# A list schedule with other durations and other ranks, in a two-layer trunk on one core

## Chip, core and metric

The kernel runs on one core of one Trainium2 chip. A core has five engines that each work through a queue of their own in program order: TensorE (PE; its weight loads are listed apart as PEld), VectorE (DVE), ScalarE (ACT), GpSimd (POOL) and SyncE (SP), which here issues nearly all DMAs. Engines wait for one another by semaphores. The metric is the device time of one execution in microseconds; lower is better.

## What is computed

Two layers over 1024 tokens of width 1024, each with three branches that share one input product, and then an output product and a gated addition:

```python
for i in range(2):
    z = rms_norm(x, norm_g[i]) @ w_in[i]
    z_a, z_b, z_c = split_cols(z, (1664, 936, 1536))
    y_a = rwkv7_branch(z_a, ...)      # a recurrence over tokens, 6 heads of 64
    y_b = dsa_branch(z_b, ...)        # the 256 best keys of each query, then attention over them, 4 heads
    y_c = dilated_branch(z_c, ...)    # banded attention at three rates, 2 heads each, joined by their lse
    x = x + concatenate([y_a, y_b, y_c]) @ w_out[i]
    gate = sigmoid(rms_norm(x, ple_norm_g[i]) @ ple_w_gate[i])
    x = x + gate * (p[i] @ ple_w_proj[i])
return rms_norm(x, final_norm_g)
```

The recurrence, per token and head, is `state = state * w + sa (kk * a) + v k`, with `sa = state @ -kk`. In `dsa_branch` the selection is a `top_k` of index scores `sum_h relu(iq_h . ik) * iw_h`.

## The kernel before

Each layer has a head (norm, transposes, the first columns of the input product), a middle that holds the three branches, and a tail (the output product and the gate). Head and tail are written out in order. The middle is not: it is some 120 Python generators ("streams"), each of which yields pieces of work, and `Flow.run` decides at build time in which order their instructions are put into the engines' queues. What it emits is fixed; nothing is rescheduled on the chip.

A stream yields `piece(engine, us)` ahead of the instructions that this piece issues, `get`/`put` for buffers (slots) that limit how far streams may run ahead, and `after`/`done` for events. `Flow.run` keeps a clock per engine. It takes the piece that can start earliest by that clock, and among pieces that can start at the same time the one of the lowest rank:

```python
self.streams.sort(key=lambda st: st["rank"])
...
start = lambda st: max(st["ready"], self.free.get(st["want"][1], 0.0))
st = min(ready, key=start)
_, engine, us, aside = st["want"]
end = self.free[engine] = start(st) + us
st["end"] = end + self.gap(st, engine)
```

`gap` is what a handover is taken to cost: one number between two pieces of a stream on one engine, and `LATENCY[engine]` from one engine to another. So the durations in the `piece` calls, the gaps and the ranks set the order, and only the order.

The streams that the change and the prediction speak of, by the lines of the profile:

- **z products** (`z_streams`, L728 to L730): the rest of the input product, 720 groups of three matmuls per layer, two PSUM banks. A bank is emptied by ACT and DVE (L748, L750, L753 for the RWKV columns, L762, L768 to L771 for the others) and then stored. Products have rank 50, the evictions 1.5. Their weights are split in two halves by ACT (L682) and POOL (L694).
- **Search** (`dsa_select`): 34 rounds of a bit-wise search for the 256th best key. A round counts keys under a threshold, for four query blocks on DVE (L572) and two on ACT (L555), and then updates the threshold on DVE (L577 to L579). Ranks 7 and, for ACT's counts, 6.
- **Mask** (`dsa_mask`, L623 to L636): six blocks of DVE work that turn the result into an additive mask, stored to DRAM. Rank 7. Its end closes the memory pools of the search; the dilated attention opens in their place.
- **RWKV**: the tokens in eight chunks (hf 0 to 7) of 128. A chunk has a preparation (`rwkv_prep`, rank 4: L1239 to L1326), products between its tokens (`rwkv_cross`, L1372 and L1376), an inverse (`rwkv_inverse`, rank 2) whose core is 31 columns of two dependent DVE operations each (L1451, L1454) that end in a transpose XT (L1462), a merge on PE (L1487, L1499), two chain steps through the state (`rwkv_chain`, rank 0: L1532 to L1559), and an output (`rwkv_out`, L1618 to L1648). Buffers hold two chunks' inverses at a time.
- **Dilated attention** (`dil_att`, from L1040 on, 24 units) with its join (`dil_join`, L1148 to L1183), and **attention over the selected keys** (`dsa_attend`, L905 to L985, ranks 29 to 34), which begins when the mask and all z products are done.
- **embedded** (rank 60, L327 to L329 into `a`): products for the tail's gate, which fill PE.

The tail (`tail`, L327 to L329 into `z`) follows the last row of the middle in each queue.

Of the kernel before, what the change touches and what calls it, by code (L numbers as in the profile page):

```python
# [34 lines left out]
RW, DS, DL = 0, 1664, 2600  # L35

# [85 lines left out]
class Flow:  # L122
# [3 lines left out]
    LATENCY = dict(PE=0.25, ACT=0.2, DVE=0.22, POOL=0.2, SP=2.4)  # L126
# [70 lines left out]
def tile_kernel(ctx, tc, x, p, norm_g, w_in, tshift_mu, rwkv_w0, rwkv_w_up, rwkv_a0, rwkv_a_up, rwkv_k_k,  # L197
# [149 lines left out]
    def dsa_index(flow, ix, zk, zp, sp_, ZT, d):  # L347
# [17 lines left out]
        def kv():  # L365
            for tp in range(0, NT, 2):
# [3 lines left out]
                for (_, zz), nm, half in zip(parts, "ri", (8, 4)):  # L370
                    yield piece("POOL", 1.0)
# [3 lines left out]
                yield piece("DVE", 0.1, True)  # L375
                DVE.tensor_scalar(iw[:, tp:tp + 2], z[:, :, 160:168], 1 / 16.0, None, OP.mult)
                yield piece("ACT", t_act(256) + t_act(128))
# [5 lines left out]
                yield piece("POOL", t_pool(128) + t_pool(64))  # L383
# [8 lines left out]
                yield piece("ACT", t_act(256))  # L392
# [19 lines left out]
        def iq():  # L412
            for tp in range(2, NT, 2):
                z = ZT["iq", tp].rearrange("p t (h e) -> p t h e", e=32)
                yield piece("POOL", 1.6)
# [7 lines left out]
                for e in range(2):  # L423
                    yield get("iqS")
                    iqS = IQ[tp + e] = ix.tile([96, 8, 128], F32R, name="iqS", bufs=2)
                    for j in range(2):
# [5 lines left out]
                        yield piece("ACT", t_act(512))  # L432
# [4 lines left out]
        def products(u):  # L437
# [6 lines left out]
            yield piece("PE", 0.02 + (c.stop - c0) / 2400)  # L444
# [5 lines left out]
        def relus(u):  # L450
            yield get("rl")
            n = B[u].shape[1]
            yield piece("ACT", 0.05 + n / 1200)
# [4 lines left out]
        def sums(u):  # L458
# [4 lines left out]
            yield piece("DVE", 0.12 + (c.stop - c0) / 960)  # L463
# [16 lines left out]
        def keys():  # L480
            for qb in range(2, NT):
# [3 lines left out]
                yield piece("ACT", 2 * t_act(n))  # L485
# [3 lines left out]
                yield piece("DVE", t_dve(n) + 0.3)  # L489
# [5 lines left out]
        def q():  # L495
            yield after("rwkv")
            ka = d["ka"]
            for tp in range(0, NT, 2):
# [5 lines left out]
                yield piece("ACT", t_act(512))  # L504
# [5 lines left out]
                for j in range(2):  # L510
# [7 lines left out]
                    yield piece("ACT", t_act(512))  # L518
# [8 lines left out]
        for g in (kv(), iq()):  # L527
            flow.add(1.7, g)
        flow.line("index", units, (2.0, products), (1.9, relus), (1.8, sums))
        flow.add(1.8, keys())  # L530
        flow.add(2.1, q())


    def dsa_select(add, mk, d):
# [13 lines left out]
        def act_counts():  # L548
            for i in range(counts):
                lower = i // (counts // 2)  # L550
                yield after("t", i)
                for qb in on_act:
                    n = (qb + 1) * 128
                    yield piece("ACT", 0.19 + n / 1080)
# [4 lines left out]
        def search():  # L559
# [7 lines left out]
            for i in range(counts):  # L567
                lower, bit = i // (counts // 2), 15 - i % (counts // 2)
                for qb in range(2, NT - COUNT_ACT):
                    n = (qb + 1) * 128  # L570
                    yield piece("DVE", 0.08 + n / 1750)
# [3 lines left out]
                yield piece("DVE", 0.35)  # L575
# [8 lines left out]
                else:  # L584
# [8 lines left out]
                    for qb in range(2, NT):  # L593
                        hi, lo = hl[qb]
                        yield piece("DVE", t_dve(200 * (qb + 1)))
# [6 lines left out]
        add(7, search())  # L602
        add(6, act_counts())

    def dsa_mask(mk, d):
# [11 lines left out]
        for qb in range(2, NT):  # L617
            n, j = (qb + 1) * 128, slice(qb - 2, qb - 1)
            hi, lo = d["hl"][qb]
            yield piece("DVE", t_dve(n))  # L620
# [4 lines left out]
            yield piece("DVE", t_dve(1.5 * n))  # L625
            DVE.tensor_tensor(bias, bias, tmp, OP.mult)
            DVE.tensor_tensor_scan(tmp, zero.to_broadcast([128, n]), bias, need[:, j], OP.add, OP.subtract)
            yield piece("DVE", t_dve(n))
            DVE.tensor_scalar(tmp, tmp, 0.0, None, OP.is_ge)
            DVE.tensor_tensor(bias, bias, tmp, OP.mult)  # L630
            for src, lim in ((hi, T), (lo, t)):
                yield piece("DVE", t_dve(n))
                DVE.tensor_scalar(tmp, src, lim[:, j], None, OP.is_gt)
                DVE.tensor_tensor(bias, bias, tmp, OP.add)
            yield piece("DVE", t_dve(n / 2))
# [1231 lines left out]
```

## Time and profile before

| | |
|---|---|
| median of three runs | 1970.13 us (1969.46 to 1970.62) |
| the profiled execution, its own time | 1973.16 us |
| its span, first to last instruction | 1971.4 us |
| PE, DVE, ACT, POOL busy, share of the span | 92%, 70%, 53%, 30% |
| middle of layer 0 | search 170 to 390, mask 395 to 483, last z product 636, first matmul of the tail 793.9 |
| middle of layer 1 | search from 1146, mask to 1456, last z product 1604, first matmul of the tail 1766 |

The spans of busy time are of one execution. Matmuls are pipelined and their ends are modelled, so a PE that reads as busy may still have room; the time from the start of one matmul to that of the next in a full stretch tells what one costs. The two layers run the same program and look alike in the trace.

### The profile page before, as it was taken

What the parts mean: (1) busy time and instruction counts of PE and PEld (TensorE: products, weight loads), DVE (VectorE), ACT (ScalarE), POOL (GpSimd) and SP (SyncE); (2) the same over time, 40 slices, a digit from 0 to 9 for tenths busy, and PEclk for the clock granted to TensorE, in tenths of its full rate; (3) what the DMA queues carried; (4) which work ended last, traced back from release to release, by engine and by line L of the source; (5) the groups of instructions that cost most, each with busy time, mean ns of one, the idle gap of its engine ahead of it and who ended that gap; (6) DMA issues with size and microseconds to landing.
All of it is one profiled execution on the core that took longest, in us unless ns stands there. A gap on an engine that the chain in (4) does not pass through costs nothing. (4 is left out here: it accounts for less than half of the span.)

```text
span 1971.4 us, 38650 instructions
## 1 busy us (share of the span) xinstructions
PE 1823.1 (92%) x14062; PEld 1666.9 (85%) x14062; DVE 1382.3 (70%) x3676; ACT 1054.1 (53%) x2393; POOL 593.8 (30%) x810
## 2 busy tenths in 40 slices
PE   7999888899999999899999988888889999999998
PEld 6887677888898888799998876787889988889998
DVE  4479999999788774215345899999996878732344
ACT  4576666543566676214246766665336667652323
POOL 5422144253222222223225212433442222212322
PEclk9999998999999999899999999989989989999999
DMA  5212232223233455612322223222242344464123
GB/s 188 70 58 82 72 96 81 64 74 111 75 99 99 146 146 160 203 44 65 108 93 69 70 73 88 79 76 67 83 118 62 106 120 135 130 197 136 47 81 114
DMA packets 232407, 196.23 MB, mean 100 GB/s; under 512 B 19284, under 2 KB 204056, under 8 KB 232216
## 3 DMA queue, kind: packets, MB, share of 16 engines
q1 hardware_dynamic: 232216, 193.75, 32.6%
q8 instruction: 111, 1.82, 0.4%
q14 instruction: 80, 0.66, 0.1%
HBM read 128.32 MB, written 65.37 MB: 98 GB/s over the span
## 5 line engine op out<-in xcount | busy, mean ns | idle before, releaser
L728 PE MATMUL z<-wH,HT 128*128 128x256 f32 x1024 | 318.8, 311 | 5.8 <-DVE zt L750 3.7
L729 PE MATMUL z<-wL,HT 128*128 128x256 f32 x1024 | 300.6, 294 | 1.3 <-POOL wL L694 1.3
L730 PE MATMUL z<-wH,LT 128*128 128x256 f32 x1024 | 299.7, 293 | 0.0
L329 PE MATMUL z<-wH,LT 128*128 128x256 f32 x1024 | 293.4, 288 | 4.1 <-DVE LT L238 4.1
L327 PE MATMUL z<-wH,HT 128*128 128x256 f32 x1024 | 290.9, 286 | 5.4 <-ACT HT L237 5.4
L328 PE MATMUL z<-wL,HT 128*128 128x256 f32 x1024 | 292.5, 287 | 0.0
L694 POOL TENSOR_TENSOR wL<-wraw,wH 128x512 fp32r<-128x512 f32 (+1 forms) x128 | 169.9, 1332 | 364.9 <-ACT wH L682 311.0
L728 PEld LDWEIGHTS z<-wH,HT 128*128 128x128 f32 x1024 | 207.2, 202 | 12.9 <-DVE zt L750 4.1
L729 PEld LDWEIGHTS z<-wL,HT 128*128 128x128 f32 x1024 | 207.5, 203 | 1.8 <-POOL wL L694 1.7
L730 PEld LDWEIGHTS z<-wH,LT 128*128 128x128 f32 x1024 | 206.6, 202 | 0.0
L329 PEld LDWEIGHTS z<-wH,LT 128*128 128x128 f32 x1024 | 198.3, 194 | 6.3 <-DVE LT L238 6.3
L327 PEld LDWEIGHTS z<-wH,HT 128*128 128x128 f32 x1024 | 198.1, 194 | 6.3 <-ACT HT L237 6.3
L328 PEld LDWEIGHTS z<-wL,HT 128*128 128x128 f32 x1024 | 198.7, 194 | 0.2
L319 POOL TENSOR_TENSOR wL<-wraw,wH 128x512 fp32r<-128x512 f32 (+1 forms) x72 | 100.3, 1413 | 295.7 <-ACT wH L318 292.5
L728 PE MATMUL z<-HT,wH 128*128 128x512 f32 x416 | 169.0, 406 | 18.0 <-DVE zt L750 9.5
L729 PE MATMUL z<-LT,wH 128*128 128x512 f32 x416 | 165.0, 397 | 0.0
L730 PE MATMUL z<-HT,wL 128*128 128x512 f32 x416 | 164.6, 396 | 0.0
L1451 DVE TENSOR_TENSOR xt<-AT,X 128x48 f32<-128x48 f32 (+20 forms) x496 | 135.7, 277 | 8.1
L1454 DVE TENSOR_TENSOR X<-X,xt 128x48 f32<-128x48 f32 (+20 forms) x496 | 124.4, 255 | 7.4
L318 ACT CAST wH<-wraw 128x512 fp32r<-128x512 f32 (+1 forms) x72 | 46.7, 652 | 133.5 <-PE z L329 92.0
L572 DVE TENSOR_SCALAR_CACHE_REDUCE junk<-hi,t 128x384 bf16<-128x384 uint16 (+3 forms) x136 | 110.4, 812 | 4.3
L728 PEld LDWEIGHTS z<-HT,wH 128*128 128x128 f32 x416 | 79.7, 192 | 38.2 <-DVE zt L750 12.0
(287 smaller groups left out, 4548.5 us busy)
## 6 DMA issues: line engine op xcount, KB each, us to landing
wraw<-in_w_in_dram SPq DMA_DIRECT2D x208, 128.0 KB
zr<-zt SPq DMA_DIRECT2D x52, 256.0 KB
zd<-zt SPq DMA_DIRECT2D x48, 256.0 KB
z<-zd SPq DMA_DIRECT2D x48, 256.0 KB
pd<-pe SPq DMA_DIRECT2D x32, 256.0 KB
wraw<-in_w_out_dram SPq DMA_DIRECT2D x32, 256.0 KB
hn<-yT SPq DMA_DIRECT2D x16, 512.0 KB
wraw<-in_ple_w_gate_dram SPq DMA_DIRECT2D x32, 256.0 KB
```

The costliest lines, as they stand in the source:

```text
L318: ACT.copy(H[:, :, :n], raw)
L319: POOL.tensor_tensor(L[:, :, :n], raw, H[:, :, :n].bitcast(F32), OP.subtract)
L327: PE.matmul(o, aH, bH, start=j == 0, stop=False)
L328: PE.matmul(o, aH, bL, start=False, stop=False)
L329: PE.matmul(o, aL, bH, start=False, stop=j == n - 1)
L572: DVE.tensor_scalar(junk[0][:, :n], hl[qb][lower], col(t, qb), None, OP.is_lt, OP.add, accum_out=col(cnt, qb))
L694: POOL.tensor_tensor(L, RAW.pop(it), H.bitcast(F32), OP.subtract)
L728: PE.matmul(o, aH, bH, start=k == 0, stop=False)
L729: PE.matmul(o, aH, bL, start=False, stop=False)
L730: PE.matmul(o, aL, bH, start=False, stop=k == 7)
L1451: DVE.tensor_tensor(tmp, AT[:, j + 1:, j:j + 1].rearrange("p t o -> p o t").to_broadcast([128, m, n]), X[:, :m, j:j + 1].to_broadcast([128 ...
L1454: DVE.tensor_tensor(X[:, :m, j + 1:], X[:, :m, j + 1:], tmp, OP.add)
```

## The change

A table of ranks, `RANK`, is set at the head of the file, and the streams take their rank from it. With it `search`, `counts` (ACT's part of the search) and `mask` get rank -1, ahead of all others, where they had 7, 6 and 7; the other ranks keep their values. The durations in some ninety `piece` calls and the gaps get other numbers. No instruction is added or removed, on any engine. Line numbers of the changed kernel are four to five higher.

```diff
+RANK = dict(chain=0, merge=1, inverse=2, cross=3, tokens=3, ahead=3, prep=4, y=5, out=6, counts=-1, search=-1, mask=-1,
+            products=50, evict=1.5, weights=1.6, embed=60, kept=35, columns=1.7, index=2.0, q=2.1, load=10, dil=20,
+            join=19, dsa=30)
...
-    LATENCY = dict(PE=0.25, ACT=0.2, DVE=0.22, POOL=0.2, SP=2.4)
+    LATENCY = dict(PE=0.2, ACT=0.14, DVE=0.12, POOL=0.13, SP=2.4)
...
-        return 0.13 if st["want"] and st["want"][0] == "piece" and st["want"][1] == engine else self.LATENCY[engine]
+        return 0.11 if st["want"] and st["want"][0] == "piece" and st["want"][1] == engine else self.LATENCY[engine]
...
-                    yield piece("DVE", 0.08 + n / 1750)
+                    yield piece("DVE", 0.17 + n / 960)
...
-                yield piece("DVE", 0.35)
+                yield piece("DVE", 0.9)
...
-        add(7, search())
-        add(6, act_counts())
+        add(RANK["search"], search())
+        add(RANK["counts"], act_counts())
...
-                        yield piece("PE", 0.645, True)
+                        yield piece("PE", 0.7, True)
...
-                yield piece("DVE", t_dve(m * n))
+                yield piece("DVE", 0.13 + m * n / 500)
...
-                yield piece("DVE", t_dve(m * n))
+                yield piece("DVE", 0.13 + m * n / 800)
...
-            flow.add(7, dsa_mask(mk, d))
+            flow.add(RANK["mask"], dsa_mask(mk, d))
```

What this does to the queues is shown at three places of layer 0's middle.

DVE's queue about the last z eviction of the RWKV columns (L750), on which the RWKV preparation waits, before. `hi_613` to `hi_619` are the keys of four query blocks, `cnt` the counts, `t` the threshold; the rows from L585 on begin the second half of the search:

```order
L572 TENSOR_SCALAR junk_634,cnt<-hi_613,t 128x384
L572 TENSOR_SCALAR junk_634,cnt<-hi_615,t 128x512
L572 TENSOR_SCALAR junk_634,cnt<-hi_617,t 128x640
L572 TENSOR_SCALAR junk_634,cnt<-hi_619,t 128x768
L750 SCALAR_TENSOR_TENSOR zt<-z,prm,zt 128x511
L585 TENSOR_TENSOR lim<-lim,cnt 128x6
L587 TENSOR_SCALAR lim<-lim 128x1 x6
L588 TENSOR_SCALAR T<-t 128x6
```

The same eviction in the changed kernel, where it is L754, the counts are L576 and the updates L581 to L583:

```order
L581 TENSOR_TENSOR step<-cnt,lim 128x6
L582 TENSOR_SCALAR step<-step 128x6
L583 TENSOR_TENSOR t<-t,step 128x6
L754 SCALAR_TENSOR_TENSOR zt<-z,prm,zt 128x511
L576 TENSOR_SCALAR junk_634,cnt<-hi_613,t 128x384
L576 TENSOR_SCALAR junk_634,cnt<-hi_615,t 128x512
L576 TENSOR_SCALAR junk_634,cnt<-hi_617,t 128x640
L576 TENSOR_SCALAR junk_634,cnt<-hi_619,t 128x768
```

The eviction moved ahead by four rounds of the search: before it stood behind the counts of all 17 rounds of the first half, now it stands behind those of 13.

DVE's queue where the columns of RWKV chunk 1 end (XT, L1462) and the mask's first block (L623 to L627) begins, before:

```order
L1451 TENSOR_TENSOR xt<-AT_1924,X 128x16
L1454 TENSOR_TENSOR X<-X,xt 128x8x2
L1618 TENSOR_REDUCE ost<-Yt 128x6
L1619 SCALAR_TENSOR_TENSOR Yt<-ost,Yt 128x384
L1451 TENSOR_TENSOR xt<-AT_1924,X 128x8
L623 TENSOR_SCALAR junk_634<-hi_613,T 128x384
L624 TENSOR_SCALAR junk_635<-lo_614,t 128x384
L1454 TENSOR_TENSOR X<-X,xt 128x8
L626 TENSOR_TENSOR junk_634<-junk_634,junk_635 128x384
L627 SCALAR_TENSOR_TENSOR junk_635<-zero,lim,junk_634 128x384
L1462 STREAM_TRANSPOSE XT<-X 128x256
```

The end of the mask's last block (`hi_623`, L640) in the changed kernel, where the same columns (now L1456 and L1459, on `AT_1898`) are at the tenth of 31, and an eviction of a late z product (L775, before L771) stands close by:

```order
L634 TENSOR_TENSOR junk_634<-junk_634,junk_635 128x1024
L1456 TENSOR_TENSOR xt<-AT_1898,X 128x69
L637 TENSOR_SCALAR junk_635<-hi_623,T 128x1024
L638 TENSOR_TENSOR junk_634<-junk_634,junk_635 128x1024
L1459 TENSOR_TENSOR X<-X,xt 128x3x23
L637 TENSOR_SCALAR junk_635<-lo_624,t 128x1024
L638 TENSOR_TENSOR junk_634<-junk_634,junk_635 128x1024
L1456 TENSOR_TENSOR xt<-AT_1898,X 128x66
L640 TENSOR_SCALAR hi_623<-junk_634 128x1024
L1459 TENSOR_TENSOR X<-X,xt 128x3x22
L1291 SCALAR_TENSOR_TENSOR kh<-zk,prm,t 128x128 x3
L775 SCALAR_TENSOR_TENSOR zt<-zt,z 128x2x128
```

The whole mask moved from behind chunk 1's columns to ahead of them, and 15 of the 16 evictions of L771 stand ahead of chunk 1's XT, where 4 stood before.

PE's queue at the end of the middle, before: the last transposes and values of the attention (L940, L963), its output (L982), and then the tail:

```order
L940 MATMUL a<-cst,pr 128x128 x4
L963 MATMUL a<-v,pT 128x64 x16
L982 MATMUL a<-cst,y 128x128 x2
L327 MATMUL z<-wH,HT 128x256
L328 MATMUL z<-wL,HT 128x256
```

And in the changed kernel, where the 24 transposes of the join stand just ahead of these rows: the merge of the last RWKV chunk (L1492, L1504), its two chain steps (L1537 to L1582), its output (L1643), and then the tail (L331):

```order
L1492 MATMUL t<-XN,G 32x32 x12
L1504 MATMUL t<-TT,rs 32x32 x12
L1537 MATMUL a<-S_1900,AR 128x128 x3
L1550 MATMUL a<-rs,TT 64x64 x6
L1560 MATMUL a<-SV,BKt 128x128 x3
L1582 MATMUL a<-SV,G 64x64 x6
L1537 MATMUL a<-S_1901,AR 128x128 x3
L1550 MATMUL a<-rs,TT 64x64 x6
L1560 MATMUL a<-SV,BKt 128x128 x3
L1582 MATMUL a<-SV,G 64x64 x6
L1643 MATMUL t<-cst,o_9179 128x128 x3
L331 MATMUL z<-wH,HT 128x256
```

The last chunk of the recurrence now ends the middle with nothing between its steps; before, attention rows stood between and behind them.

## Rows read from the trace of the kernel before

**Rows 1.** The page: busy time of each engine, and DVE's and PE's busy tenths in 40 slices of 49.3 us.

```profile
PE 1823.1 (92%) x14062; PEld 1666.9 (85%) x14062; DVE 1382.3 (70%) x3676; ACT 1054.1 (53%) x2393; POOL 593.8 (30%) x810
PE   7999888899999999899999988888889999999998
DVE  4479999999788774215345899999996878732344
```

**Rows 2.** Busy time by stretch, layer 0: the first half of the search, the second half and the mask, from there to the XT of RWKV chunk 7, from there to the tail's first matmul; and sums of these.

```profile
core 0: us, PE busy (x) PEld busy (x) DVE busy (x) ACT busy (x) POOL busy (x), PEclk, DMA share, GB/s
170.00:254.00 84.00, 72.09 (x324) 57.99 (x322) 77.58 (x203) 53.88 (x97) 18.93 (x24) 0.98 0.27 79
254.00:491.00 237.00, 206.13 (x1713) 195.94 (x1714) 224.71 (x649) 119.11 (x260) 91.79 (x130) 0.91 0.28 81
491.00:726.60 235.60, 223.69 (x2121) 204.21 (x2119) 186.75 (x656) 152.18 (x449) 56.00 (x72) 0.96 0.36 108
726.60:793.90 67.30, 64.89 (x521) 53.78 (x520) 30.63 (x86) 42.55 (x90) 16.22 (x18) 0.99 0.53 161
170.00:793.90 623.90, 566.80 (x4675) 511.92 (x4673) 519.66 (x1591) 367.72 (x895) 182.93 (x244) 0.95 0.34 100
```

**Rows 3.** The same for the answering stretches of layer 1.

```profile
1229.00:1464.00 235.00, 202.36 (x1714) 192.39 (x1715) 225.45 (x653) 119.52 (x261) 93.50 (x130) 0.93 0.29 83
1464.00:1699.00 235.00, 222.93 (x2116) 203.75 (x2115) 185.89 (x653) 152.22 (x449) 55.72 (x72) 0.96 0.36 107
```

**Rows 4.** What PE waited for between 170 and 254 us: us in total, times, longest.

```profile
PE z L728 <- DVE last L753: 5.3, 4, 2.5
PE z L728 <- DVE zt L750: 4.8, 3, 1.7
```

**Rows 5.** DVE's groups between 170 and 390 us (busy us, mean ns | idle before), those of the search and of RWKV's columns.

```profile
L572 DVE TENSOR_SCALAR_CACHE_REDUCE junk<-hi,t 128x384 bf16<-128x384 uint16 (+1 forms) x68 | 55.2, 812 | 2.1
L1451 DVE TENSOR_TENSOR xt<-AT,X 128x60 f32<-128x60 f32 (+24 forms) x55 | 15.7, 287 | 0.3
L1454 DVE TENSOR_TENSOR X<-X,xt 128x60 f32<-128x60 f32 (+24 forms) x54 | 14.3, 267 | 0.3
```

**Rows 6.** PE in two stretches of 25 us that it filled, with z products 512 wide and with products 256 wide: the count of matmuls stands behind its busy time.

```profile
150.00:175.00 25.00, 25.00 (x111) 20.47 (x110) 22.07 (x33) 17.00 (x29) 7.01 (x13) 1.00 0.28 83
850.00:875.00 25.00, 25.00 (x211) 25.00 (x210) 2.95 (x5) 3.99 (x7) 6.70 (x6) 1.00 0.13 43
```

**Rows 7.** The z products of L728 alone (one of the three matmuls of a group) from 170 us on: PE and PEld busy with them, and counts.

```profile
170.00:254.00 84.00, 41.54 (x108) 20.50 (x107) 0.98 0.27 79
254.00:491.00 237.00, 114.91 (x370) 76.16 (x370) 0.91 0.28 81
491.00:640.00 149.00, 40.26 (x127) 24.74 (x126) 0.95 0.31 92
```

**Rows 8.** The XT of RWKV chunks 1 and 4: start, duration, engine, line.

```profile
397.38 0.42 DVE L1462 STREAM_TRANSPOSE XT<-X 128x256 f32<-128x256 f32 x1
580.88 0.45 DVE L1462 STREAM_TRANSPOSE XT<-X 128x256 f32<-128x256 f32 x1
```

**Rows 9.** RWKV chunk 7 from its XT to its last row, in order of time: start, duration, engine, line (other rows between them left out).

```profile
726.12 0.45 DVE L1462 STREAM_TRANSPOSE XT<-X 128x256 f32<-128x256 f32 x1
...
732.00 0.63 ACT L1503 COPY TT<-t 32x192 f32<-32x192 f32 x2
...
737.27 0.89 PE L1532 MATMUL a<-S,AR 128*128 128x128 f32 x6
...
743.32 0.74 DVE L1559 TENSOR_TENSOR S<-a,sp 64x192 f32<-64x192 f32 x2 [0.34 <-PE a L1555]
...
746.40 0.94 PE L1532 MATMUL a<-S,AR 128*128 128x128 f32 x6
...
752.38 0.74 DVE L1559 TENSOR_TENSOR S<-a,sp 64x192 f32<-64x192 f32 x2 [0.24 <-PE a L1555]
753.15 0.56 DVE L1579 TENSOR_TENSOR Yt<-a,rs 64x384 f32<-64x384 f32 x1
...
758.48 0.56 DVE L1632 TENSOR_TENSOR o<-Yt,ost 128x384 f32<-128x384 f32 x1
...
761.13 0.50 PE L1638 MATMUL t<-cst,o 128*128 128x128 f32 x3
...
764.19 0.55 DVE L1648 SCALAR_TENSOR_TENSOR o<-o,zg 128x384 f32<-128x384 f32 x1
```

**Rows 10.** The end of the middle and the tail's first matmuls, in order of time.

```profile
792.46 0.37 ACT L985 COPY yt<-a 128x256 f32<-128x256 f32 x1 [4.30 <-PE a L982]
793.85 0.58 PE L327 MATMUL z<-wH,HT 128*128 128x256 f32 x1 [1.43 <-ACT HT L237]
797.20 0.41 PE L329 MATMUL z<-wH,LT 128*128 128x256 f32 x1
797.41 0.41 PE L327 MATMUL z<-wH,HT 128*128 128x256 f32 x1
...
800.55 0.28 PE L328 MATMUL z<-wL,HT 128*128 128x256 f32 x1
800.67 0.28 PE L329 MATMUL z<-wH,LT 128*128 128x256 f32 x1
```

**Rows 11.** DVE's columns of one chunk, and POOL, about 552 us; and POOL's splits of z weights (L694) between 491 and 640 us: busy time and count.

```profile
551.61 0.21 DVE L1451 TENSOR_TENSOR xt<-AT,X 128x30 f32<-128x30 f32 x1
551.85 0.19 DVE L1454 TENSOR_TENSOR X<-X,xt 128x30 f32<-128x30 f32 x1
552.08 0.97 DVE L1451 TENSOR_TENSOR xt<-AT,X 128x29 f32<-128x29 f32 x1
553.08 0.19 DVE L1454 TENSOR_TENSOR X<-X,xt 128x29 f32<-128x29 f32 x1
552.00 1.00 POOL L1645 TENSOR_TENSOR o<-o,t 128x384 f32<-128x384 f32 x1 [3.39 <-ACT o L1641]
491.00:640.00 149.00, 8.30 (x6) 0.95 0.31 92
```

More of the change, by code (lines that the diff above doesn't have):

```diff
@@ L527, in dsa_index @@
         for g in (kv(), iq()):
[L528 to L531, printed above, removed]
+            flow.add(RANK["columns"], g)
+        flow.line("index", units, *((RANK["index"] - 0.1 * k, f) for k, f in enumerate((products, relus, sums))))
+        flow.add(RANK["index"] - 0.2, keys())
+        flow.add(RANK["q"], q())
     def dsa_select(add, mk, d):
@@ L993, in dsa_attend @@
         units = [(qb, h, c0) for qb in range(NT) for h in range(4) for c0 in range(0, (qb + 1) * 128, 512)]
-        flow.line("qload", range(NT), (10, load))
-        flow.line("dsa", units, (32, scores), (33, biased), (30, softmax))
-        flow.line("dsb", units, (31, transposes), (31, turned), (34, values))
-        flow.line("dso", range(NT), (29, output))
+        flow.line("qload", range(NT), (RANK["load"], load))
+        flow.line("dsa", units, *((RANK["dsa"] + k, f) for k, f in ((2, scores), (3, biased), (0, softmax))))
+        flow.line("dsb", units, *((RANK["dsa"] + k, f) for k, f in ((1, transposes), (1, turned), (4, values))))
+        flow.line("dso", range(NT), (RANK["dsa"] - 1, output))
     hrow = lambda h: slice(h % 2 * 64, h % 2 * 64 + 64)
@@ L1128, in output @@
                 yield done("dil")
-        flow.line("dil", units, (10, load), (24, turn), (24, turned), (23, scores), (23, biased), (22, softmax),
-                  (21, transposes), (21, weights), (20, values), (20, output))
+        flow.line("dil", units, (RANK["load"], load), *((RANK["dil"] + k, f) for k, f in (
+            (4, turn), (4, turned), (3, scores), (3, biased), (2, softmax), (1, transposes), (1, weights), (0, values),
+            (0, output))))
     def dil_join(opened):
@@ L1268, in icl @@
             lora, wa, ta, ke = R["lora"], T["wa"], tile_("ta"), tile_("ke")
-            yield from product(lambda pr: lora[64:, fc(pr)], lambda pr: wa[64:], "ACT", 3 * t_act(128), tanh(ta, "a0"))
-            yield piece("DVE", 3 * t_dve(128) + t_dve(384))
+            yield from product(lambda pr: lora[64:, fc(pr)], lambda pr: wa[64:], "ACT", 0.8, tanh(ta, "a0"))
+            yield piece("DVE", 1.6)
             for pr in range(3):
@@ L1643, in rwkv_out @@
         yield put("t")
-        yield piece("POOL", t_pool(384))
+        yield piece("POOL", 1.07)
         POOL.tensor_tensor(dv, dv, R["t2"], OP.add)
         yield put("t2")
-        yield piece("DVE", t_dve(384))
+        yield piece("DVE", 0.52)
         DVE.scalar_tensor_tensor(dv, dv, 0.5, g, OP.mult, OP.mult)
```

194 lines of the change are left out of this document (97 added, 97 removed).

## The prediction

> **What bounds the kernel now.** I read the page first. PE is busy for 92% of the span, but DVE's tenths show where the kernel changes character: nines from slice 4 on for a third of each layer, then less [rows 1]. So next came the busy time by stretch. Between 170 and 491 us (search, mask, the first two RWKV chunks) DVE is at 92% and 95%; between 491 and 726.6 it falls to 79% [rows 2], and layer 1 repeats this [rows 3]. In the first part DVE is the bound; even so PE waits there for evictions that stand in DVE's queue behind counts [rows 4]. In the second part no engine is full: what limits it is the chain through the RWKV chunks, which begins late. PE's 95% there is not a bound, since its ends are modelled: in full stretches a matmul 512 wide costs 25/111 = 0.225 us and one 256 wide 25/211 = 0.118 [rows 6], and the 127 rows of L728 between 491 and 640 us, 127 x 0.118 = 15 us of work, read as 40 us busy [rows 7]. The middle ends at 793.9 with the attention [rows 10], 29 us behind the last RWKV row [rows 9].
>
> Since no instruction is added or removed, the change can only reorder. Head and tail stay as they are. So I need the new end of the middle, once, and count it twice.
>
> **What the reordering does, part by part.** The index scores up to 170 us keep their order almost row for row: nothing there. Then three things move.
>
> (1) The evictions of z step ahead of the search's counts, as the first place of the order shows. This answers PE's waits of 10.1 us [rows 4] and lets the z products run ahead: in the new order nearly all of them stand before chunk 1's merge, and DVE has 15 of the 16 late evictions ahead of chunk 1's XT where it had 4. The first stretch therefore ends when both engines are through, and I count each up to chunk 1's XT.
> PE: the rows of L728 from 170 us on are 108 + 370 + 127 = 605 [rows 7], of which 512 are 256 wide and 93 are 512 wide, each times three: 512 x 3 x 0.118 + 93 x 3 x 0.225 = 181 + 63 = 244 us. Ahead of the merge the new order has 280 other matmul rows, at about 0.11 (half the 512-wide price, for shapes up to 128 wide) 31. Together 275. At 95% (a choice between the 206/237 = 87% that PE shows in the second row [rows 2] and full) that is 290.
> DVE: from 170 to 491 it did 77.6 + 224.7 = 302 us [rows 2], which hold the search, the mask and the columns of chunks 0 to 2. Chunk 2's columns, 31 x (0.287 + 0.267) = 17 [rows 5], and, as an estimate, about as much again of the preparation and outputs of chunks 2 to 4 now come later. That leaves some 270, at the 92% of the first row 292.
> Both come to about 291, and two engines that are both full wait for each other; I add 9. **Chunk 1's XT at 470.** By the old order it was at 397 [rows 8], with the mask and most z products still to come.
>
> (2) Search and mask go first. This costs RWKV its slots there: chunk 1 waits for the whole mask, as the second place shows. By the order some 98 DVE rows, about 30 us, lie between the mask's end and that XT, so the mask ends near 440 instead of 483 and gives the dilated attention its memory 40 us earlier; the attention over the selected keys can start when z ends, near 480 instead of 638. Both are filler for the later stretch. The work itself is the same: 68 counts of 0.812 us in the first half [rows 5] and as many in the second.
>
> (3) What is left is RWKV chunks 2 to 7 with the two attentions. DVE does 519.7 us from 170 to 793.9 [rows 2]. Behind the last XT the new order has only the chunk's own chain and output, 8 us (thirteen operations of 0.55 to 0.74 [rows 9]). So 512 - 270 = 242 us of DVE lie between the XT of chunk 1 and that of chunk 7. The old rows bound the speed: 79% where chains and z products shared PE, 95% where DVE had free choice [rows 2]. PE has 244 us of z products behind it by then and none can stand ahead of a chain step, which speaks for the upper end; nearly all of DVE's work there is two chunks' chains, which speaks for the lower. I take the middle, 87%: 242/0.87 = 278, **chunk 7's XT at 748**.
>
> (4) The third place: behind that XT nothing covers the last chunk. Its length from its own rows [rows 9]: XT to the end of TT's copy 6.5; the two chain steps 744.1 - 737.3 = 6.8 and 753.1 - 746.4 = 6.7, with 0.5 between; Yt to the last row 11.6, less 2.1 in which the transposes stood behind attention rows, 9.5. Together 30. The tail follows at 778 where it began at 793.9 [rows 10]: **16 us per layer, 32 for both.** Where the chain has to share its engines as it did before, it took 38.6; that is one end of this term.
>
> Against the profiled execution's 1973.2 us this gives 1941. It lies 3 us above the median of 1970.1, so I predict 1938 as the median of runs. Differences within 0.2%, 4 us, I count as none: that is about what a measurement here can tell.
>
> One rule speaks against (4). In the tail's first stretch matmuls start 0.21 us apart at 797.2, and 0.12 apart at 800.6 [rows 10]: after a pause PE was at the lower of its two clock levels, 1.2 GHz. The Trainium skill says the same (TensorE: Matmul & The Clock Gate, "What's actually happening"): the gate halves the clock when the array has been idle and returns it when it is busy. By that rule the new uncovered chain would run its matmuls at half clock: about 6.5 us of its 30 are PE's, so 6 us more per layer, and the sum would be 1950 instead of 1938. The sum above takes the rows at full clock.
>
> **The rivals.**
> (a) *The second stretch keeps its old pace* (the slower side). If the chain through two chunks sets it, DVE stays at 79%: 242/0.793 = 305, XT at 775, tail at 805, 11 us later per layer, 1992. For it: the only row of such a stretch says 79%, and from the XT of chunk 4 to that of chunk 7 it took 726 - 581 = 145 us for three chunks [rows 8, 9]. Against it: PE and attention stood in the way there. It decides from 242/(793.9 - 30 - 470) = 82% downwards.
> (b) *PE bounds the first stretch.* At the 87% of the old row, 275/0.87 = 316, XT of chunk 1 at 486 or later; with the rest as above the middle ends at 794, no change; with (a) on top 2025.
> (c) *The whole middle runs at DVE's 95%.* 512/0.948 = 540, XT at 710, tail at 740, 54 earlier per layer: 1862. For it: all of search, columns, dilated and attention are at hand for DVE at any time. Against it: the chain waits between engines.
> (d) *POOL holds DVE.* A column took 0.97 us instead of 0.20 while POOL worked on one of its own [rows 11]. POOL's splits for z now fall in the search stretch: from 491 to 640 there were six [rows 11], 6 x 0.77 = 5 us per layer at most, 10 in all, if each holds one operation. The forecast would be 1948.
>
> **Numbers.** Forecast with (d) and the half clock as its upper part, 1915 to 1958: 0.47. Stronger gains up to (c): 0.15. No change, by (b) alone or by half of (a): 0.10. Slower, by (a) or by (a) and (b): 0.28. Range for eight in ten: 1895 to 2000, which leaves out (c)'s end and (a) with (b); the forecast's own range is 1915 to 1958. Faster by over 0.2%: 0.62; within: 0.10; slower: 0.28.
>
> **What would show each step.** (1) the last z product near 480 instead of 636 and PE's waits for `zt` and `last` gone; (2) the mask's end near 440 instead of 483; (3) DVE near 87% between the XTs of chunks 1 and 7 in place of 79%; (4) the last row of RWKV as the last of the middle, some 30 us behind its XT, with PE nearly idle. The forecast is wrong if DVE's share between these XTs is under 82%, or if chunk 1's XT comes after 490.

## The result, and the profile after

The changed kernel takes 1992.8 us (median of four runs, 1986.4 to 1999.1) against 1969.8 (1967.9 to 1970.6): a ratio of 1.0118, interval 1.008 to 1.0155. It is 23 us slower where 32 us less had been forecast. The execution below is one of the four, 1999.1 us with a span of 1997.3.

The page of the kernel after, to be read beside [rows 1]:

```profile
span 1997.3 us, 38612 instructions
...
PE 1840.6 (92%) x14062; PEld 1683.0 (84%) x14062; DVE 1380.3 (69%) x3676; ACT 1060.6 (53%) x2393; POOL 598.9 (30%) x810
...
PE   7999989999999994899999999899999999759998
...
DVE  4489989897877883215445899998888868722344
...
PEclk9999999999889895899999999999998877959999
```

The busy sums are nearly those of before; the time is in holes. PE has a 4 at the end of the first middle (slice 16) and a 7 and a 5 at the end of the second (35 and 36). The clock row falls to 5 there and lies at 8 and 7 in most slices just ahead.

Busy time by stretch of the kernel after: the first half of the search, then from 171 us to the XT of chunk 1, from there to that of chunk 7, from there to RWKV's last row, to the tail's first matmul, the tail's first 31 us, and in layer 1 again from the XT of chunk 1 to that of chunk 7. Columns as in [rows 2].

```profile
170.00:254.00 84.00, 84.00 (x467) 73.37 (x466) 77.14 (x214) 59.54 (x111) 25.13 (x32) 1.00 0.33 100
171.00:472.00 301.00, 286.56 (x2206) 270.42 (x2204) 269.70 (x735) 170.91 (x354) 111.90 (x147) 0.98 0.33 99
472.00:762.00 290.00, 264.59 (x2326) 229.40 (x2326) 234.17 (x829) 188.68 (x517) 70.64 (x89) 0.89 0.32 97
762.00:790.00 28.00, 15.02 (x128) 12.35 (x126) 7.47 (x16) 7.24 (x17) 3.69 (x5) 0.56 0.08 29
790.00:799.00 9.00, 0.00 (x0) 0.00 (x0) 0.44 (x1) 1.04 (x1) 0.00 (x0) 0.50 0.86 233
799.00:830.00 31.00, 23.67 (x140) 22.27 (x141) 8.79 (x8) 9.64 (x10) 7.47 (x4) 0.78 0.96 300
1457.00:1752.00 295.00, 271.32 (x2329) 235.02 (x2328) 234.59 (x830) 188.94 (x518) 70.66 (x89) 0.87 0.32 95
```

Up to chunk 1's XT DVE is busy for 90%, and that XT comes where forecast. From there to chunk 7's XT it is 234.2/290 = 81%, nearly the old 79% [rows 2]. Behind it come 28 us in which PE is busy for 15 and no other engine for more than 8, and 9 us with next to nothing on PE, DVE, ACT or POOL.

The kernel after in order of time, layer 0: the XTs of chunks 1, 4 and 7, the first chain step's matmuls, RWKV's last row, its store, the tail's first load and split, and its first matmul.

```profile
471.54 0.44 DVE L1467 STREAM_TRANSPOSE XT<-X 128x256 f32<-128x256 f32 x1
614.94 0.45 DVE L1467 STREAM_TRANSPOSE XT<-X 128x256 f32<-128x256 f32 x1
762.01 0.45 DVE L1467 STREAM_TRANSPOSE XT<-X 128x256 f32<-128x256 f32 x1
766.34 1.65 PE L1537 MATMUL a<-S,AR 128*128 128x128 f32 x6
789.88 0.56 DVE L1653 SCALAR_TENSOR_TENSOR o<-o,zg 128x384 f32<-128x384 f32 x1 [3.31 <-POOL o L1650]
790.46 0.36 SPq L1655 DMA_DIRECT2D yT<-o  x1
791.46 0.39 SPq L1666 DMA_DIRECT2D hn<-yT  x1
797.93 1.04 ACT L241 CAST HT<-hn 128x1024 fp32r<-128x1024 f32 x1 [9.16 <-DMA hn<-yT]
799.03 0.58 PE L331 MATMUL z<-wH,HT 128*128 128x256 f32 x1 [11.45 <-ACT HT L241]
```

The six matmuls of a chain step take 1.65 us here and 0.89 in [rows 9], which is the half clock. The tail's first load stands behind RWKV's last store, and the first matmul 8.6 us behind RWKV's last row (790.44); before, 1.0 us lay between the attention's last copy and that matmul [rows 10], since there RWKV was through 28 us ahead of that copy and the first load stood just behind RWKV's last store, under the attention:

```profile
764.77 0.36 SPq L1650 DMA_DIRECT2D yT<-o  x1
768.49 1.38 SPq L1661 DMA_DIRECT2D hn<-yT  x1
```

### The profile page after: what moved, and what is told of

It is laid out like the page before. It is cut to its first block, busy times and chain, and to the rows that moved or that the text cites. A ratio compares the mean times of both kernels' runs of the same rounds, so it can differ in the third digit from the quotient of the medians.

```text
span 1997.3 us, 38612 instructions
## 1 busy us (share of the span) xinstructions
PE 1840.6 (92%) x14062; PEld 1683.0 (84%) x14062; DVE 1380.3 (69%) x3676; ACT 1060.6 (53%) x2393; POOL 598.9 (30%) x810
## 5 line engine op out<-in xcount | busy, mean ns | idle before, releaser
L331 PE MATMUL z<-wH,HT 128*128 128x256 f32 x1024 | 292.9, 288 | 29.8 <-ACT HT L241 29.8
L732 PE MATMUL z<-wH,HT 128*128 128x256 f32 x1024 | 301.1, 294 | 0.0
L333 PE MATMUL z<-wH,LT 128*128 128x256 f32 x1024 | 294.7, 289 | 4.2 <-DVE LT L242 4.2
L733 PE MATMUL z<-wL,HT 128*128 128x256 f32 x1024 | 292.7, 286 | 6.1 <-POOL wL L698 6.1
L332 PE MATMUL z<-wL,HT 128*128 128x256 f32 x1024 | 294.0, 288 | 0.0
L734 PE MATMUL z<-wH,LT 128*128 128x256 f32 x1024 | 292.1, 285 | 0.0
L331 PEld LDWEIGHTS z<-wH,HT 128*128 128x128 f32 x1024 | 199.9, 196 | 31.4 <-ACT HT L241 31.2
L733 PEld LDWEIGHTS z<-wL,HT 128*128 128x128 f32 x1024 | 198.8, 194 | 7.3 <-POOL wL L698 7.3
L333 PEld LDWEIGHTS z<-wH,LT 128*128 128x128 f32 x1024 | 200.0, 196 | 5.9 <-DVE LT L242 5.9
L732 PEld LDWEIGHTS z<-wH,HT 128*128 128x128 f32 x1024 | 198.7, 194 | 3.5 <-issue 0.4
L332 PEld LDWEIGHTS z<-wL,HT 128*128 128x128 f32 x1024 | 200.5, 196 | 0.1
L734 PEld LDWEIGHTS z<-wH,LT 128*128 128x128 f32 x1024 | 198.6, 194 | 0.0
L1456 DVE TENSOR_TENSOR xt<-AT,X 128x54 f32<-128x54 f32 (+22 forms) x496 | 126.6, 262 | 5.8
L1459 DVE TENSOR_TENSOR X<-X,xt 128x54 f32<-128x54 f32 (+22 forms) x496 | 125.0, 258 | 5.5
L576 DVE TENSOR_SCALAR_CACHE_REDUCE junk<-hi,t 128x384 bf16<-128x384 uint16 (+3 forms) x136 | 110.3, 811 | 3.8
L576 DVE TENSOR_SCALAR_CACHE_REDUCE junk<-lo,t 128x384 bf16<-128x384 uint16 (+3 forms) x136 | 109.5, 805 | 0.2
```

Of the source, the lines that this page charges most:

```text
L331: PE.matmul(o, aH, bH, start=j == 0, stop=False)
L332: PE.matmul(o, aH, bL, start=False, stop=False)
L333: PE.matmul(o, aL, bH, start=False, stop=j == n - 1)
L576: DVE.tensor_scalar(junk[0][:, :n], hl[qb][lower], col(t, qb), None, OP.is_lt, OP.add, accum_out=col(cnt, qb))
L732: PE.matmul(o, aH, bH, start=k == 0, stop=False)
L733: PE.matmul(o, aH, bL, start=False, stop=False)
```

## The experiments

The kernel after is the base of all of them but the first. Totals are medians, with the ratio to the kernel before and its interval; lengths of stretches are from one profiled execution of each, and a pair of lengths is layer 0 and layer 1. That execution can lie some way from the median: it took 1999.1 us for the kernel after, the longest of four.

**Which part of the change.** The ranks alone, and the times alone.

```
- add(7, search()); add(6, act_counts()); flow.add(7, dsa_mask(mk, d))
+ add(-1, search()); add(-1, act_counts()); flow.add(-1, dsa_mask(mk, d))
```

> The kernel before, its old times per piece, with search, counts and mask at rank -1. If the three ranks alone bring the loss (they put RWKV behind the whole search), this run has the mask's end near 440 us, chunk 1's XT near 470, RWKV last in each middle, and takes 1985 to 2005 us. If the measured times per piece bring it, this run stays at 1965 to 1975.

```
- counts=-1, search=-1, mask=-1
+ counts=6, search=7, mask=7
```

> The kernel after with the old ranks of search (7), counts (6) and mask (7): the measured times alone. If the ranks alone bring the loss, this run has chunk 1's XT back near 400 us, z products still running at 600, attention last, and takes 1960 to 1975 us. If the measured times bring it, by letting z products run ahead, it takes 1985 to 2000.

The ranks alone took 1984.0 us (1.0063, 1.004 to 1.0085), the times alone 2126.8 (1.0792, 1.0771 to 1.0813). The first lies between its two expectations, with the mask's end at 427 and chunk 1's XT at 444 in an execution of 1970.4 us, the shortest of ten; the second is outside both. Two stretches of the run with the times alone, around the XT of chunk 7:

```profile
500.00:654.00 154.00, 81.63 (x680) 69.72 (x679) 135.66 (x446) 48.41 (x115) 33.41 (x43) 0.64 0.17 49
654.00:867.00 213.00, 179.08 (x1276) 152.06 (x1274) 68.35 (x267) 122.89 (x360) 25.19 (x24) 0.88 0.39 118
```

The z products are through at 507 us, but the mask only at 643; the dilated attention, which needs its memory, waits for it. PE is busy for 53% of the 154 us ahead of that XT, and DVE for 32% of the 213 behind it. So the new durations make the ranks necessary: with them the ranks are worth 134 us, with the old durations they cost 14. With the ranks alone the middle of layer 0 ends at 792.1 with the attention, RWKV being through at 773.6.

**The clock.** One bf16 matmul into each PSUM bank as it is taken up, from the end of the z products to the end of the middle, 128 and then 384 columns wide; real matmuls overwrite it.

```
+ def warmed(b):
+     if warm: PE.matmul(b[:, :128], reset[:, :128], reset[:, :128], start=True, stop=True)
+     return b
- return bank("a", 4)          (and z, t)
+ return warmed(bank("a", 4))
```

> The kernel after, with one bf16 matmul of 128 columns written into each PSUM bank as it is taken up, ahead of the real matmuls that overwrite it, from the end of the z products to the end of the middle: 706 of them, about 20 us of PE per layer at full clock. Theory of the clock: PE is at half clock for about a fifth of the stretch 472 to 762 us and all of 750 to 800, because no z products are left; with the added matmuls the granted clock of the stretch goes from 0.89 to 0.95 or more, chunk 7's XT comes at 745 to 752 instead of 762, and the run takes 1955 to 1980 us. Theory of the chain: two chunks' steps from engine to engine set the pace whatever the clock; the XT stays at 760 or later and the run takes 1990 to 2010.

> The same with 384 columns each: about 56 us of PE per layer at full clock. Theory of the clock: the granted clock goes to 0.97 or more; the run takes 1950 to 1985 us, less than the kernel after, though PE has more to do. Theory of the chain: the added work stands in the way of the chain, and the run takes 2010 to 2040 us.

They took 2014.9 us (1.0229, 1.0212 to 1.0246), more than either theory had, and 2037.7 (1.0347, 1.033 to 1.0364), in the range of the theory of the chain. The stretch between the XTs of chunks 1 and 7 with 128 columns, then with 384, then chunk 7's own stretch with 384:

```profile
469.00:768.00 299.00, 281.43 (x2679) 244.54 (x2679) 233.32 (x836) 189.89 (x518) 69.41 (x89) 0.93 0.32 95
```

```profile
473.00:789.00 316.00, 299.28 (x2672) 250.31 (x2671) 233.08 (x832) 191.01 (x517) 69.23 (x89) 0.96 0.30 89
789.00:817.00 28.00, 17.29 (x139) 12.67 (x137) 7.20 (x15) 7.14 (x17) 3.33 (x5) 0.68 0.08 29
```

The clock of the stretch rose from 0.89 to 0.93 and 0.96, nearly as far as the theory of the clock said, and the stretch grew, 290 to 299 and 316. What the clock gives back there is less than the added matmuls cost.

**The clock at the bare end alone.** Five matmuls of 384 columns in each bank of the last chunk and 50 behind its last transposes (45, and the five of that bank).

> The kernel after, with bf16 matmuls of 384 columns written into each PSUM bank that the last chunk takes up, five ahead of its real matmuls, and 45 behind its last transposes: work in PE's waits between chunk 7's XT and the tail alone. Theory of the clock at the bare end: PE is granted 0.56 there and 0.78 in the tail's first 31 us; at full clock the chunk's 28.5 us become 22 to 24 and the tail's start wins 2 to 4, so 8 us per layer, 1972 to 1982 us. Rival: the waits between engines set the chunk's length at either clock, 1988 to 1998.

1992.1 us (1.0124, 1.0092 to 1.0155), as the kernel after and as the rival said. From chunk 7's XT to RWKV's last row, and on to the tail:

```profile
753.00:782.00 29.00, 22.11 (x184) 15.22 (x183) 8.08 (x17) 7.25 (x17) 3.70 (x5) 0.79 0.08 29
782.00:790.00 8.00, 7.67 (x42) 4.13 (x39) 0.00 (x0) 0.95 (x1) 0.00 (x0) 0.88 0.78 253
```

At 0.79 in place of 0.56 the chunk still takes 29 us. The added matmuls can also stand ahead of a real one, so this shows that no time is to be won there by such means, and does not price the clock by itself.

**The loads.** First the tail's first tiles in memory that others leave earlier.

```
- outer = pool(cur, "to", "right"); tw.default = pool(cur, "ti", "right")
- tw.pools.update({n: outer for n in "xb hn gb gbn".split()})
+ tw.default = pool(cur, "ti", "right"); wide, outer = pool(cur, "tx", "right"), pool(cur, "to", "right")
+ tw.pools.update(xb=wide, hn=outer, gbn=outer)        (and a pad that moves them out of RWKV's memory)
```

> The kernel after, with the tail's first tiles (hn, the norm's gain gbn and x) laid into memory that the dilated attention and its join leave, in place of RWKV's. The first load of yT then stands ahead of RWKV's last store in SP's order, the second not yet. Theory of the loads: the 8.6 us between RWKV's last row (790.5) and the tail's first matmul (799.0) come from that load alone; they shrink to about 2, 7 us per layer, and the run takes 1978 to 1986 us. Rival: the next loads set the tail's start-up anyway, so what is won at its first matmul is lost by its fourth tile; 1988 to 1995.

1987.0 us (1.0071, 1.0051 to 1.0092), between its two ranges; with 6 us between the medians and 13 between single runs of the kernel after, this alone says little. In layer 0 the tail's first tile ran inside the chunk's waits, but the wait came back one tile later:

```profile
797.58 0.36 SPq L1655 DMA_DIRECT2D yT<-o  x1
798.52 0.44 SPq L1666 DMA_DIRECT2D hn<-yT  x1
...
805.04 0.58 PE L331 MATMUL z<-wH,HT 128*128 128x256 f32 x1 [10.35 <-ACT HT L241]
```

Then seven tiles of yT ahead of the store, in three buffers of their own (`yl`), and last the first four tiles of x too.

```
- yt = tw.tile([128, 8, 128], F32, name="hn", bufs=2)
+ yt = tw.tile([128, 8, 128], F32, name="yl", bufs=3)     (in a pool of its own, where dil and join were)
- SP.dma_start(xb[:, h], src[tk])
+ (behind the loop over h)
```

> The kernel after, with a pool of three buffers of its own for the tail's loads of yT, in memory that the dilated attention and its join leave; the loads of x come behind all of them. Seven of the eight tiles now stand ahead of RWKV's last store in SP's order, and the tail's splits and first products stand between the steps of the last chunk on ACT, DVE and PE. Theory of the bare end: the 8.6 us of loads go, and up to two PSUM banks of products (four tiles, 96 matmuls of 0.12, some 11 us of PE) move into the chunk's waits: 12 to 20 us per layer, 1955 to 1970 us. Rival: the splits wait for their loads ahead of chain steps on ACT and DVE and stretch the chunk by as much: 1985 to 1995.

```
- xb = tw.tile([128, NT, D], F32, name="xb")
+ xb = [tw.tile([128, 2, D], F32, name=f"xb{j}") for j in range(NT // 2)]     (xb0, xb1 in the pool of yl)
+ for g in {3: (0, 1), 5: (2, 3), 7: (4, 5, 6, 7)}.get(h, ()):
+     SP.dma_start(xb[g // 2][:, g % 2], src[g * 128:g * 128 + 128])
```

> The run with seven tiles loaded early, and also the first four tiles of x, in memory beside theirs and ahead of RWKV's last store. There PE stood 13 us at the tail's third PSUM bank, since DVE's addition waited for x, loaded behind that store. Theory of the bare end: those 13 us go too, at least 8 of them per layer, and the run takes 1940 to 1958 us. Rival: DVE's additions now stand between the last chunk's steps and stretch it, or PE's products do: 1962 to 1975.

1970.0 us (0.9997, 0.9977 to 1.0016), at the upper end of the range of its theory, and 1949.0 (0.990, 0.9864 to 0.9937), within it. What PE waited for longest in the first of them, from 755 to 840 us:

```profile
PE z L331 <- DVE xb L1680: 13.0, 1, 13.0
```

The second run has no such wait; its longest there is 8.5 us for the split of a later tile:

```profile
PE z L331 <- ACT HT L241: 8.5, 1, 8.5
```

Its stretches from chunk 7's XT to RWKV's last row, and on to 830 us:

```profile
756.00:798.00 42.00, 35.95 (x297) 33.49 (x296) 17.35 (x28) 14.45 (x25) 4.57 (x5) 0.79 0.60 171
798.00:830.00 32.00, 23.87 (x180) 23.58 (x181) 5.12 (x7) 7.03 (x9) 13.20 (x8) 0.84 0.67 218
```

The chunk itself got longer, 42 us for 28, with the tail's splits and products between its steps; but PE does 297 matmuls in it for 128, and the tail is already under way. Filling the bare end was worth 44 us between the medians, and this version beats both kernels.

**Filler for the bare end.** The embedding's last three column blocks and the attention of the last three query tiles are held back by gates on the chunks.

```
+ (embedded) g = [None, 4, 5, 6][n];  if g is not None: yield after("chain", g)
+ (scores) if qb >= 5: yield after("chain", 5 if qb == 5 else 6)
```

> The kernel after, with filler held back by gates on the RWKV chunks: the embedding's last three column blocks wait for the chain of chunk 4, 5 and 6, the attention of query tile 5 for that of chunk 5 and tiles 6 and 7 for that of chunk 6. Theory of the bare end: in the kernel after 37 us of each layer, from chunk 7's XT to the tail, have PE and DVE nearly idle (28.5 of chain and 8.6 of loads), and the same filler stood in the chain's way earlier. Held back it fills that end: RWKV is through by 775, the attention ends 5 to 15 us behind it, the loads are hidden, and the run takes 1950 to 1975 us. Rival: PE and DVE are needed in full for filler and chain alike, so that RWKV gains nothing and the filler comes on top of it: 1990 or more.

1994.1 us (1.0107, 1.0083 to 1.0131): no gain, as the rival said, though not for its reason, since RWKV did come forward. From the XT of chunk 1 to that of chunk 7, to RWKV's end, to the tail:

```profile
470.00:738.00 268.00, 236.61 (x2011) 202.08 (x2010) 212.62 (x788) 164.11 (x468) 58.95 (x79) 0.84 0.33 97
738.00:773.00 35.00, 33.28 (x282) 24.65 (x283) 22.16 (x56) 22.25 (x46) 7.43 (x10) 0.95 0.04 13
773.00:794.00 21.00, 19.10 (x170) 18.66 (x168) 2.44 (x7) 11.57 (x23) 5.81 (x6) 1.00 0.76 244
```

RWKV's last XT came 24 us earlier, the loads were hidden, and the filler ran 20 us past RWKV's end with DVE at 2.4 of 21 us: the hole changed sides. In the profiled executions orders as unlike as that of before, this one, and that of the ranks alone all reach the tail of layer 0 between 792 and 795 us; of the last two the shortest execution was profiled.

**What one us of each engine counts** in the stretch between the XTs of chunks 1 and 7. The three edits leave the order as it is.

```
- for k in range(m): PE.matmul(O[qb]..., start=k0 + k == 0, stop=k0 + k == qb)
+ for k in range(m):
+     if k0 + k == qb: PE.matmul(O[qb]..., start=True, stop=True)
```

> The kernel after without most of the products of probabilities and values (224 of 288 matmul rows per layer, some 25 us of PE at 0.11 each); the output is that of the last key block alone. The planner's durations and so every order stay. If PE's time sets the pace between the XTs of chunks 1 and 7 one for one, that stretch falls from 290 to 265 us and the run takes 1940 to 1950 us. By the added matmuls of the run with 384 columns (26 us longer for 56 us of work) it falls by 12: 1965 to 1975. If neither counts but only the chain's own steps, it stays at 285 to 290 and the run takes 1985 to 1995.

```
+ for _ in range(2):
      DVE.tensor_tensor_reduce(PR[qb, h][:, kc], ...)
```

> The kernel after with each score tile's biased copy on DVE done twice, with the same result: 56 operations of 0.28 to 0.68 us and as many reads of the accumulator, some 30 us of DVE per layer. The planner's durations and so every order stay. If DVE's time sets the pace between the XTs of chunks 1 and 7 one for one, that stretch grows from 290 to 320 us and the run takes 2045 to 2055 us; if it counts by half, 2015 to 2030; if the chain's own steps set it, 1990 to 2003.

```
+ for _ in range(2):
      ACT.copy(PT[it][:, :t.shape[1]], t)
```

> The kernel after with each copy of the transposed probabilities on ACT done twice, with the same result: some 56 copies, mostly of 0.59 us, 25 us of ACT per layer, most of it between the XTs of chunks 1 and 7. The planner's durations and so every order stay. If that stretch is made of work handed from engine to engine, with little slack on any, it grows by 8 to 18 us, as it did for DVE and PE, and the run takes 2008 to 2030 us. If ACT, busy for 65% of it, has slack, it grows by under 4 us: 1990 to 2000.

1982.8 us (1.0061, 1.0037 to 1.0085), 2035.1 (1.0327, 1.0296 to 1.0357) and 2016.5 (1.024, 1.0193 to 1.0288); the first two lie between the ranges expected, the third in the first of its two. The stretch in layer 0, less PE, more DVE, more ACT:

```profile
470.00:751.00 281.00, 240.68 (x2110) 203.24 (x2109) 235.26 (x834) 188.32 (x518) 71.08 (x89) 0.89 0.34 101
```

```profile
471.00:779.00 308.00, 275.78 (x2325) 237.31 (x2325) 258.13 (x924) 189.33 (x517) 69.72 (x89) 0.87 0.31 91
```

```profile
471.00:774.00 303.00, 276.45 (x2330) 238.59 (x2329) 234.76 (x831) 209.62 (x565) 70.56 (x89) 0.86 0.31 93
```

In both layers it is 281 and 283 us, 308 and 315, 303 and 297, against 290 and 295. Per us of work that is 10.5/25 = 0.4 for PE, 19/24 = 0.8 for DVE and 7.5/21 = 0.4 for ACT, on average of the layers. These are rough. The same stretch, with nothing in it edited, differs by as much from one profiled execution to the next, as in the run with matmuls at the bare end (both layers) and in the first run on the loads (layer 0):

```profile
469.00:753.00 284.00, 258.71 (x2330) 224.31 (x2329) 233.77 (x830) 188.73 (x517) 70.74 (x89) 0.91 0.33 99
1449.00:1740.00 291.00, 267.15 (x2330) 232.52 (x2330) 234.51 (x832) 188.78 (x517) 70.73 (x89) 0.88 0.32 97
```

```profile
470.00:769.00 299.00, 274.60 (x2331) 238.03 (x2329) 234.55 (x831) 188.92 (x518) 71.23 (x89) 0.86 0.32 94
```

Half of the difference between the medians, which is the change per layer, gives 5.0/25 = 0.2 for PE, 21.2/24 = 0.9 for DVE and 11.9/21 = 0.6 for ACT. So added work on DVE counts nearly in full and on ACT by about half; PE counts least, and how much is not settled.

**Much less filler.** The attention over the selected keys cut to 128 keys for each query tile, in the same order; then with the bf16 matmuls of 384 columns beside it.

```
- m = kc.stop - c0            (scores; likewise biased, softmax, transposes, turned, values)
+ if c0: return
+ m = 128
```

> The kernel after with the attention over the selected keys cut to the first 128 keys for each query tile (its output is not the reference's); the planner's durations and so every order stay. Per layer this takes away some 50 us of PE, 21 of DVE and 27 of ACT, nearly all between the XTs of chunks 1 and 7. If that stretch is made of work handed between the engines, each counting as the runs with more DVE, less PE and more ACT said (0.7, 0.4 and 0.5 us for one us), it falls from 290 to 240 to 250 us and the run takes 1895 to 1915 us. If the chain through the chunks has a floor of its own near the present pace, it stays at 272 or more and the run takes 1955 or more.

> The run with the cut attention (its output is not the reference's) and the bf16 matmuls of 384 columns in each PSUM bank together. The cut attention took 50 us of PE, 15 of DVE and 25 of ACT per layer away, and the stretch between the XTs of chunks 1 and 7 fell by 11 us alone, while its granted clock fell from 0.88 to 0.80. The added matmuls give PE about as much work as it had. Theory of the clock: it took the gain back, and the added matmuls bring it to 0.95 or more; what DVE and ACT won then shows, the stretch falls to 250 to 268 us, the run to 1915 to 1950. Theory of a floor: the chain's own hand-overs hold the stretch at 275 or more whatever the clock; 1965 to 2000.

1973.7 us and 1981.9, both in the range of the theory of a floor. The stretch in layer 0 of both:

```profile
471.00:759.00 288.00, 239.00 (x1976) 211.33 (x1975) 221.00 (x810) 164.35 (x503) 71.62 (x89) 0.78 0.33 98
```

```profile
470.00:756.00 286.00, 253.15 (x2271) 212.76 (x2270) 216.84 (x797) 164.08 (x501) 70.99 (x89) 0.92 0.33 98
```

With the cut attention it is 287 and 275 us, with the matmuls beside it 286 in both layers: at a clock of 0.92, with DVE at 76% and ACT at 57%, it is hardly shorter than the 290 and 295 with all the work. But the second run does not price the clock, since its added matmuls cost time as well. With these matmuls in both runs, the cut attention takes the stretch from 316 and 313 us to 286, 28 us per layer; without them it takes off 3.5 and 20, by the medians 10 per layer.

Two readings are left. Either the hand-overs along the chain of chunks hold the stretch near 280 in this order, whatever stands between them; or the clock, which fell to 0.78, took back part of what the cut attention gave. These runs do not part the two. A floor would be one of this order and not of the work: the run with filler held back took 268 and 272, with a clock of 0.84 in layer 0. Which of the hand-overs sets the pace was not tried and stays open.

## Why the prediction was wrong

**Step 1 was right.** Chunk 1's XT came at 471.5, forecast 470; the last z product began at 479, forecast near 480; and from 170 to 254 us PE was busy for all 84 us, with 467 matmuls for 324 [rows 2], so that the waits of [rows 4] are gone. Rival (b) falls with it. DVE's work up to that XT was sized well, 269.7 us for 270; the 9 us added for mutual waiting had no row behind them, and that they came out is luck.

**Step 2 was right.** The mask's last operation starts at 434.7, forecast near 440.

**Step 3 failed, in the speed.** The step took DVE's share for the pace, "the middle, 87%", between an old row at 79% and one at 95%. The work was sized well, 234 us for 242; the share was 81%, and the stretch took 290.5 us for 278. This is rival (a), and below the 82% from which it decides. A share of DVE says little where two chunks' steps are handed from PE to ACT to DVE and back, on queues that keep their order: the run with cut attention and added matmuls keeps the pace at a DVE share of 76%, and work added on DVE or ACT lengthens the stretch. Why the share is 81% and not more stays open, as said above. The pace itself stood in the prediction, under rival (a): three chunks took 145 us from the XT of chunk 4 to that of chunk 7, so six would take 290. In the kernel after, chunks 1 to 4 took 143.4 us and chunks 4 to 7 147.1. Nothing in the chain spoke for a quicker one.

**Step 4 was right on the chunk and missed the loads.** From XT to RWKV's last row took 28.4 us, forecast 30, with PE busy for 15 of 28. "The tail follows at 778" supposed that the tail's first matmul stands ready, as it did at 793.9 [rows 10]. There RWKV had ended 28 us earlier: its memory was free, and the loads of yT were issued under cover of the attention, the first at 768.5. Once RWKV is last, the loads stand behind its last store in SP's order: 8.6 us from its last row to the tail in layer 0, 8.2 in layer 1, a term that the sum put at nothing. The prediction looked at what covers the last chunk, but not at which queue holds what behind the new last instruction.

**The half clock.** PE was granted 0.56 in the bare chunk, so 1.2 GHz for most of it, and its rows are nearly twice as long (1.65 for 0.89). In the 9 us behind it, in which PE does nothing, the granted clock is 0.50. The Trainium skill (TensorE: Matmul & The Clock Gate, "What's actually happening") says so of an idle array, and the trace agrees. The matmuls of the two chain steps took 8.5 us (1.65, 1.54 and 1.65, then 1.44, 0.91 and 1.28) where a group takes 0.89 to 0.91 at the higher level, so some 3 us there are the half clock's. They did not come on top: the 30 had been read from rows in which the chain shared its engines [rows 9], and the steps as a whole took 7.4 and 6.2 us, for 6.8 and 6.7. That the chunk's 28.4 us come so near to 30 is thus two errors that cancel, the clock left out and waits for other rows counted in. The run with matmuls at the bare end found no time to win.

**Counting a layer twice.** Of the 16 us forecast for layer 0, 5.5 came from the search's first step, at 170.8 instead of 176.3. In layer 1 that step comes 359.2 us behind the tail's first matmul of layer 0, before 357.8; what is won there has no second copy. From that step to the tail before took 615.1 us, and by the forecast's own steps 607.2: 8 us were to be had, not 16.

The profiled execution took 1999.1 us and the sum was 1941. The 58 us between them are, but for rounding: 21.0 in layer 0's middle (1.5 of step 1, 12.5 of step 3, -1.6 of the chunk, 8.6 of loads), 22.7 in layer 1's (629.9 us from the search's first step to the tail, for 607.2), 8.0 of the layer counted twice, 1.4 between the layers, and 4.6 in the last tail (209.2 us for 204.6). The first 31 us of that tail, after and before:

```profile
1788.00:1819.00 31.00, 27.34 (x185) 26.64 (x186) 11.78 (x11) 7.39 (x8) 0.00 (x0) 0.82 0.84 272
```

```profile
1766.80:1797.80 31.00, 30.26 (x223) 29.19 (x224) 12.20 (x12) 9.06 (x10) 3.67 (x3) 0.91 0.67 216
```

There are 38 matmuls fewer, 38 x 0.12 = 4.6 us, at a lower clock and with fewer tiles loaded ahead.

Beside the kernel before, whose profiled execution was 26 us shorter, the loads make the larger part: 8.6 and 8.2 us where 1.0 lay, 15 for both layers, and 5 in the last tail. Up to RWKV's last row, with the same 1.0 us behind it, layer 0's middle would end 2 us earlier than before, and layer 1's, counted from the search's first step, is 8 us longer. So the gain was missing by step 3 and by the layer counted twice, and the bare loads made most of the loss.

Rival (a) gave 1992 and the runs gave 1992.8, but not by its terms alone: its stretch is longer than the measured one (305 for 290.5), and it has no loads. Against (c), DVE was busy for 90% and then 81%, for its 95%; against (d), DVE's busy time is 1380.3 us for 1382.3, so POOL cannot have held it for 10 us more than before. That the bare end is real and worth filling is what the last run on the loads shows: with the same order up to chunk 7's XT, 1949.0 us.

## What to carry to other kernels

Where a stretch is a chain handed between engines with filler beside it, no engine's busy share is its pace: take the old pace of the nearest such stretch, in us per step of the chain, and change it only for a reason in the chain. When a change makes another piece of work the last, look at once at what stands behind it in each queue and whose memory it holds; loads that were hidden for free are then bare, and the time is better filled by starting the next stage early than by saving filler for the end. Add up a layer that repeats from its own first instruction, not from a fixed time.

## What the runs showed of the hardware

Single runs of the kernels with long thin stretches lie far apart, and nearly in the order of their mean granted clock: the kernel after took 1986.4, 1989.3, 1996.2 and 1999.1 us at 0.941, 0.939, 0.934 and 0.933, and the fastest version 1940.1 to 1967.7 at 0.955 to 0.940. The stretch between the XTs of chunks 1 and 7, where nothing in it was edited, goes the same way in the profiled executions: 284 us at 0.91, 290 at 0.89, 295 at 0.87, 299 at 0.86. Of the kernel before, thirteen runs beside the first experiments lay between 1967.6 and 1972.9 at 0.958 to 0.971, and four with 384 added columns between 2036.9 and 2042.1 at 0.964 to 0.971. Whether the clock makes those runs longer, or longer waits lower the clock, is not settled: raising it by added matmuls won nothing here.
